# Ten weight-stationary matmul groups turned to activation-stationary, heads let in by the landing of their operands, and two output groups woven

## The chip, the cores and the metric

The kernel runs on one core of a Trainium2 chip. The metric is device time in microseconds (us) of one execution. In the rows, PE is the matrix engine and PEld its weight loads, DVE the vector engine, ACT the scalar engine, POOL and SPq two engines that here mostly issue DMAs; L95 is line 95 of the kernel before.

## The reference

Two layers over 256 positions of width 2048. A layer is one wide input projection, three kinds of head, a gate on each, one output projection and a layer norm:

```python
h = x @ w_in                       # (256, 2048) @ (2048, ...), split:
a_q, a_k, a_v, a_z, b_q, b_k, b_v, b_z, b_lr, m_q, m_z = jnp.split(h, cuts, axis=-1)
y_a = chunk_band_attention(a_q, a_k, a_v, rel_table)      # 8 heads of 128, softmax with a bias
o_b = gla_chunk_recurrence(b_q, b_k, b_v, log_g)          # 4 heads, gated linear attention, chunks of 64
y_b = o_b * lax.rsqrt(mean(o_b**2) + RMS_EPS) * gla_norm_g
y_m = memory_attention(m_q, *split(mem @ w_mem_kv))       # 4 heads of 128 into 256 memory rows
y = concatenate([y_a * silu(a_z), y_b * silu(b_z), y_m * silu(m_z)])
x = layer_norm(DEEPNORM_ALPHA * x + y @ w_out, ln_g, ln_b)
```

All arrays are float32.

## The kernel before

**Products.** Every big product is made in three parts, so as to keep float32 precision with inputs rounded for the matrix engine: an operand is split into `hi` (rounded) and `lo` (the rest), and the product is hi·hi + lo·hi + hi·lo. The activations are split once per layer into `x` tiles (`xq`: four quarters of the contracted dimension; a quarter holds hi and lo side by side, 2×256 columns).

**Pieces.** The weights are streamed. A `piece` is 2×128 rows of the contracted dimension by 512 columns, or 4×128 by 256: 128x1024 elements in a tile. SP loads it into a `raw` tile, ACT copies the rounded half to `wh` (L117), DVE subtracts and writes `wl` (L118). `raw`, `wh` and `wl` have four buffers each, so piece n can be split only when PE has done with piece n−4. The pieces carry a high priority for the scheduler that orders ACT, DVE and POOL; PE and SP run in the order in which the code is written.

**Two forms of a group.** A group is eight pieces, one tile of the PSUM (`acc`) and 512 output columns. `as_group` (activation-stationary): for each row block of 128 and each half of the 256 positions, three matmuls (hi·wh, lo·wh, hi·wl) with 512 weight columns streamed: a step of 3×512 columns. `ws_group` (weight-stationary): for each row block two matmuls of 512 columns (the stationary block of `wh` with hi and lo side by side) and two of 256 (`wl` with hi): a step of 2×512 + 2×256 columns. The weight-stationary form gives the result with channels on the partitions, which is what heads and gates want; the other gives positions on the partitions.

**Turning.** `turned` brings an activation-stationary result to channels on the partitions: DVE transposes 32x32 blocks into a scratch tile (L521), POOL sends it home to DRAM (L523) and reads it back block row by block row, four DMAs for each half (L526). `placed` then copies the landed blocks to their place. Before, the queries (AQ0, AQ1, MQ) take this way, the attention keys (AK0, AK1) and the gates (AZ0, AZ1, MZ) are weight-stationary, the gates with `total` (adding the two halves) and Silu.

**Order of work.** A layer is: memory keys and values; BQK; four value groups `values(0..3)` of 388 columns, with AQ0 and AK0 after `values(2)` and AQ1 and AK1 after `values(3)`; MQ; BZ; AZ0, AZ1, MZ; then four output groups WO. Beside the groups run the heads, written as Python generators: the linear attention (`gla`), eight attention heads (`a_head`: scores QK, bias, softmax, transposed probabilities `pT` by the way of `turned`, then PV on PE) and four memory heads (`m_head`, whose probabilities are also split, `sc<-pT`). `tick()` is called after each piece: it lets waiting heads in (two or three at a time) and runs a generator whose due time has come, at most one step each tick; a generator yields the number of ticks until it is due again. `finish(gens)` calls `tick` until those are done.

Of the kernel before, what the change touches and what calls it, by code (L numbers as in the profile page):

```python
# [8 lines left out]
F32 = mybir.dt.float32  # L9
# [27 lines left out]
def hybrid_trunk_kernel(  # L37
# [9 lines left out]


    ctx.enter_context(tc.manual_schedule(engines={PE, mybir.EngineType.SP}))
    waiting, active, done, now, linear = [], [], set(), [0], []  # L50
# [103 lines left out]
    def first_pieces(p, x):  # L154


        xsrc, j0 = memT[p // 2], p % 2 * 2
        xraw = early[:, p // 2]
        vsrc = w512[0, G_MV, p].rearrange("p (k n) -> p k n", k=2)
        ksrc = w512[0, G_MK, p // 2:8:4, :, j0 * 256:j0 * 256 + 512].rearrange("h p (k n) -> p k h n", k=2)  # L160
        raws, his, los = ([wp.tile([P, 2, 512], dt, name=nm(n), tag=n) for _ in range(2)]
                          for n, dt in (("raw", F32), ("wh", F32R), ("wl", F32R)))

        def x_part(j):
            sp.dma_start(xraw[:, j], xsrc[:, j])  # L165
            parts(x[0][:, j], x[1][:, j], xraw[:, j])

        def split(i, at):
            parts(his[i][at], los[i][at], raws[i][at])

        if p < 2:
            with tc.manual_schedule(engines={DVE, mybir.EngineType.Activation}):
                for k in range(2):
                    x_part(slice(j0 + k, j0 + k + 1))
                    cut = 2 if p == k == 0 else 1
                    for h in range(cut):
                        cs = slice(h * 512 // cut, (h + 1) * 512 // cut)
                        sp.dma_start(raws[0][:, k, cs], vsrc[:, k, cs])  # L178
                        split(0, (slice(None), k, cs))
# [12 lines left out]
    def first_memory(mk, mv, each):  # L192
# [5 lines left out]

        def values_of(p, w, kk):

            for h in range(2 if p == kk == 0 else 1):
                cs = slice(h * 256, h * 256 + 256) if p == kk == 0 else slice(0, 512)
                for t in range(2):
                    as_products(accv[:, t, cs], t, memq, [x[:, :, cs] for x in w], p * 2 + kk, kk, -1 if h else 0)

        def keys_of(p, w, kk):
            (wh, wl), (xh, _, both), j = w, memq[p // 2], p % 2 * 2 + kk
# [90 lines left out]
    def gla_inputs(l):  # L298

        gw = sm.tile([P, 256], F32R, name=nm("gw"), tag="gw")  # L300
        raw = hd.tile([48, 256], F32, name=nm("gwraw"), tag="pairs0")
        gb = small([P, 2], "gb")
        ng = small([P, 1], "ng")
        for i in range(3):
            pool.dma_start(raw[i * 16:i * 16 + 16], gate_w[l])  # L305
        pool.memset(gw.bitcast(F32), 0.0)
        tc.keep_in_program_order(act.copy(gw[:48], raw))
        tc.keep_in_program_order(dve.tensor_tensor(gw[32:48], raw[32:], gw[32:48].bitcast(F32), op=ALU.subtract))
        pool.dma_start(gb, gate_b[l])
        pool.dma_start(ng, norm_g[l])  # L310
        return gw, gb, ng

    def gla(gw, gb, ng, gq, gk, lr, asv, yraw):
# [178 lines left out]
    def gla_turned(yraw, ng, y):  # L492

        yT = []
        for par in range(2):
            yT.append(hd.tile([P, 4, P], F32, name=nm("yT"), tag=("gq", "gk")[par]))
            turned(P, (yT[par], yraw[:, 2 * par:2 * par + 2].rearrange("p t d -> p (t d)")))
            yield 6
        for par in range(2):
            for t in range(2):  # L500
                for b in range(2):
# [6 lines left out]
    def placed(raw, place):  # L508

        for t in range(2):  # L510
            place(raw[:, t].rearrange("p a (g j) -> p g a j", j=32),
                  lambda x: x[:, :, t * P:(t + 1) * P].rearrange("p g (a j) -> p g a j", j=32))
        return
        yield

# [14 lines left out]
    def a_head(h, load_bias, bias, q, k, asv, y):  # L530
# [1 line left out]
        if h + 2 < 8:  # L532
            load_bias(h + 2)
        pb = bank()
        mm(pb[:, 0:128], q[:, 0:128], k[:, 0:128], True, True)
        mm(pb[:, 128:384], q[:, 128:256], k, True, True)
# [238 lines left out]
    zeros = hd.tile([P, P], F32, name="zeros", tag="st")  # L775
    dve.memset(zeros, 0.0)
    idle = bank()
    for _ in range(6):
        mm(idle[:, :P], zeros, zeros, True, True)

    res = per.tile([P, 2, D], F32, name="res")
# [3 lines left out]
    for l in range(L):  # L785
        def halves(g):
            return [[w512[l, g, h * 4 + pc // 2][:, pc % 2 * 512:pc % 2 * 512 + 512] for h in range(2)] for pc in range(8)]

        def staged(g, x, raw, place):
# [3 lines left out]
            gen = placed(raw, place)  # L793
# [77 lines left out]
        for half in range(2):  # L871
            values(2 + half)
            q = hd.tile([P, 4, T], F32, name=nm("qk"), tag="qk", bufs=4)
            laid = staged(G_AQ0 if half == 0 else G_AQ1, xq, yraw[3], lambda src, at, q=q: act.copy(at(q), src))
            k = heads(G_AK0 if half == 0 else G_AK1)
            finish(laid)
            gens.append([a_head(half * 4 + h, load_bias, bias, q[:, h], k[:, h], asv, yraw[1 + half][:, h]) for h in range(4)])
            waiting.extend(gens[-1])
        q = [hd.tile([P, 4, T], F32R, name=nm("mq"), tag="qk", bufs=4) for _ in range(2)]
        laid = staged(G_MQ, xq, yraw[3], lambda src, at: parts(at(q[0]), at(q[1]), src))  # L880
        gens.append([m_head(h, q, mk, mv, yraw[3][:, h], laid) for h in range(4)])
        waiting.extend(gens[-1])


        acc = as_group(halves(G_BZ), xq, 512)
# [1 line left out]
        gla_gate(acc, yraw[0])  # L887
        yq = [operand()]
        gens[0] = [gla_turned(yraw[0], gp[2], yq[0])]
        waiting[:0] = gens[0]  # L890
        for i, g in ((1, G_AZ0), (2, G_AZ1), (3, G_MZ)):
            y = operand()
            gates = []
            for j, a, b in ws_group(w512[l, g], xq):
                sz = scratch([P, 2, T])
                total(sz, a, b)
                act.activation(sz, sz, AF.Silu)
                gates.append((j, sz))
            finish(gens[i])
            for j, sz in gates:  # L900
                dve.tensor_tensor(sz, sz, yraw[i][:, j:j + 2], op=ALU.mult)
                parts(y[0][:, j:j + 2], y[1][:, j:j + 2], sz)
            yq.append(y)
        finish(gens[0])


        last = l == L - 1
        stats = small([P, 2, 2 * WO_N, 6], "stats")
        gb = []
        rows = norm_rows(l) if last else None  # L910
        for n in range(WO_N):
            if last:
                g, b = scratch([P, 512]), scratch([P, 512])
            else:
                both = per.tile([P, 2, 512], F32, name=nm("gb"), tag=f"yr{n}")
                g, b = both[:, 0], both[:, 1]
            pool.dma_start(g, ln_g[l:l + 1, columns(n)].to_broadcast([P, 512]))
            pool.dma_start(b, ln_b[l:l + 1, columns(n)].to_broadcast([P, 512]))
            gb.append((g, b))
            src = wo_pieces(l, n)  # L920
            if last and n == WO_N - 1:

# [22 lines left out]

                norm_last(accs, rest, stats, gb, rows, more)
                break
            acc = as_group(src, yq, 512)
            for t in range(2):
                add_residual(n, t, acc[:, t], stats)  # L950
            if last:
                r = res[:, 1, columns(n)]
                dve.tensor_tensor(r, r, gb[n][0], op=ALU.mult)
        if not last:
            norm_between(stats)
            gbT = norm_columns(l)

# [85 lines left out]
```

## Time and profile before

| | |
|---|---|
| median of 3 runs (lowest, highest) | 910.96 us (910.96, 911.66) |
| the profiled execution | 911.12 us; its span 909.3 us, 1.8 us lie outside |
| granted PE clock | 0.998 of full speed |
| PE busy | 902.5 us, 99% of the span, 5116 instructions |
| DVE, ACT, POOL busy | 606.7, 486.0, 148.1 us |
| DMA | 200.86 MB, mean 221 GB/s |

The span is what the rows show, from the first instruction to the last. A row of a group of instructions is: line, engine, operation, out<-in with the shape of a tile, count | busy us, mean ns of one | idle us of that engine just ahead of them, and what ended it. A timeline row is: start us, duration us, engine, line, operation, count in the row, and in brackets the idle time ahead of it with its releaser.

### The profile page before, as it was taken

What the parts mean: (1) busy time and instruction counts of PE and PEld (TensorE: products, weight loads), DVE (VectorE), ACT (ScalarE), POOL (GpSimd) and SP (SyncE); (2) the same over time, 40 slices, a digit from 0 to 9 for tenths busy, and PEclk for the clock granted to TensorE, in tenths of its full rate; (3) what the DMA queues carried; (4) which work ended last, traced back from release to release, by engine and by line L of the source; (5) the groups of instructions that cost most, each with busy time, mean ns of one, the idle gap of its engine ahead of it and who ended that gap; (6) DMA issues with size and microseconds to landing.
All of it is one profiled execution on the core that took longest, in us unless ns stands there. A gap on an engine that the chain in (4) does not pass through costs nothing.

```text
span 909.3 us, 14115 instructions
## 1 busy us (share of the span) xinstructions
PE 902.5 (99%) x5116; PEld 783.0 (86%) x5116; DVE 606.7 (67%) x865; ACT 486.0 (53%) x708; POOL 148.1 (16%) x279
## 2 busy tenths in 40 slices
PE   9999999999999999999999999999999999999997
PEld 7889998998888888888888899889888888888885
DVE  5765478757566666655587676885756586876566
ACT  5654475474544666533476445754744365663340
POOL 1002002014142232000000220021141431420000
PEclk9999999999999999999999999999999999999999
DMA  8977875668786778756775687666696966696552
GB/s 292 315 229 213 303 222 185 184 206 272 213 238 215 234 221 257 229 197 195 225 249 177 197 242 209 195 195 208 193 282 192 271 208 212 209 295 212 190 162 93
DMA packets 109365, 200.86 MB, mean 221 GB/s; under 512 B 12136, under 2 KB 72936, under 8 KB 109040
## 3 DMA queue, kind: packets, MB, share of 16 engines
q1 hardware_dynamic: 97920, 173.31, 60.5%
q0 software_dynamic: 11232, 26.40, 10.2%
q8 instruction: 40, 0.66, 0.3%
q10 hardware_dynamic: 144, 0.26, 0.1%
q14 instruction: 29, 0.24, 0.1%
HBM read 186.78 MB, written 13.11 MB: 220 GB/s over the span
## 4 chain that ended last, share of the span: by engine, by line
PE 98%; DMA 1%; SPq 0%; DVE 0%; ACT 0%; issue 0%
PE acc L95 90%; PE bk L95 8%; DMA raw<-w 1%; PE bk L615 0%; SPq L178 0%; PE bk L398 0%; SPq L165 0%; ACT res L771 0%; ACT wh L117 0%; DVE stats L756 0%; PE bk L345 0%; SPq L180 0%; DVE res L755 0%; DVE res L707 0%; DVE mvt L710 0%
## 5 line engine op out<-in xcount | busy, mean ns | idle before, releaser
L95 PE MATMUL acc<-wh,x 128*128 128x512 f32 (+2 forms) x1812 | 538.8, 378 | 0.0
L118 DVE TENSOR_TENSOR wl<-raw,wh 128x1024 fp32r<-128x1024 f32 (+3 forms) x321 | 369.4, 1153 | 207.6 <-ACT wh L117 205.7
L117 ACT CAST wh<-raw 128x1024 fp32r<-128x1024 f32 (+3 forms) x321 | 318.5, 994 | 315.2 <-PE acc L95 244.9
L95 PEld LDWEIGHTS acc<-wh,x 128*128 128x128 f32 x1812 | 334.9, 189 | 48.9 <-issue 0.3
L95 PE MATMUL acc<-wl,x 128*128 128x512 f32 (+2 forms) x906 | 340.8, 376 | 0.0
L95 PE MATMUL acc<-x,wh 128*128 128x512 f32 x672 | 212.2, 397 | 0.1
L95 PEld LDWEIGHTS acc<-wl,x 128*128 128x128 f32 x906 | 170.5, 188 | 26.4 <-DVE wl L118 0.6
L95 PEld LDWEIGHTS acc<-x,wl 128*128 128x128 f32 x672 | 126.2, 188 | 29.7
L95 PE MATMUL acc<-x,wl 128*128 128x256 f32 x672 | 132.2, 278 | 0.0
L95 PEld LDWEIGHTS acc<-x,wh 128*128 128x128 f32 x672 | 103.7, 189 | 1.7 <-ACT wh L117 0.5
L523 POOL DMA_DIRECT2D home<-sc x46 | 25.7, 558 | 397.3 <-DVE sc L521 390.6
L526 POOL DMA_DIRECT2D pT<-home x96 | 52.6, 554 | 51.4 <-DMA home<-sc 29.9
L526 POOL DMA_DIRECT2D yr<-home x48 | 26.1, 551 | 15.1 <-issue 8.0
L545 ACT ACTIVATE sc<-sc,mx 128x128 f32<-128x128 f32 (+1 forms) x32 | 14.4, 450 | 17.2 <-DVE mx L543 17.2
L305 POOL DMA_DIRECT2D gwraw<-gate_w x6 | 3.1, 522 | 105.7 <-PE bk L603 104.9
L387 ACT ACTIVATE sc<-sc 128x512 f32<-128x512 f32 x12 | 7.6, 633 | 14.9 <-DVE sc L385 14.9
L521 DVE STREAM_TRANSPOSE sc<-sc 128x384 f32<-128x384 f32 (+1 forms) x24 | 14.9, 619 | 0.5
L538 DVE SCALAR_TENSOR_TENSOR sc<-bk,bias 128x384 f32<-128x384 f32 x16 | 8.7, 544 | 9.1 <-PE bk L95 9.1
L521 DVE STREAM_TRANSPOSE sc<-acc 128x512 f32<-128x512 f32 x18 | 11.8, 696 | 3.6 <-PE acc L95 3.4
L118 DVE TENSOR_TENSOR x<-sc,x 128x512 fp32r<-128x512 f32 x20 | 13.5, 685 | 0.7 <-ACT x L117 0.7
L526 POOL DMA_DIRECT2D qk<-home x24 | 13.1, 552 | 5.0 <-DMA home<-sc 5.0
L118 DVE TENSOR_TENSOR x<-res,x 128x512 fp32r<-128x512 f32 (+2 forms) x14 | 10.5, 765 | 5.1 <-ACT x L117 5.1
(211 smaller groups left out, 601.0 us busy)
## 6 DMA issues: line engine op xcount, KB each, us to landing
raw<-w SPq DMA_DIRECT2D x142, 512.0 KB, 4.4
raw<-w SPq DMA_DIRECT2D x227, 256.0 KB, 4.0
raw<-w SPq DMA_DIRECT2D x64, 388.0 KB, 3.7
home<-sc POOLq DMA_DIRECT2D x30, 256.0 KB, 4.0
bias<-relw SPq DMA_DIRECT2D x16, 192.0 KB, 4.7
yr<-home POOLq DMA_DIRECT2D x48, 64.0 KB, 4.9
home<-sc POOLq DMA_DIRECT2D x16, 192.0 KB, 3.3
pT<-home POOLq DMA_DIRECT2D x64, 48.0 KB, 4.3
```

The source lines that it names most:

```text
L95: pe.matmul(o, l, r, start=start, stop=stop, skip_group_check=True)
L117: act.copy(hi, src)
L118: dve.tensor_tensor(lo, src, hi.bitcast(F32), op=ALU.subtract)
L305: pool.dma_start(raw[i * 16:i * 16 + 16], gate_w[l])
L387: act.activation(dd, dd, AF.Abs)
L521: dve.transpose(blocks.rearrange("p b (g j) -> p g b j", j=32), src.rearrange("p (g b j) -> p g b j", b=4, j=32))
L523: pool.dma_start(homes[-1], blocks)
L526: pool.dma_start(dst[b * 32:(b + 1) * 32], home[:, b].rearrange("(a i) n -> i a n", a=4))
L538: dve.scalar_tensor_tensor(s, pb[:, :384], SCALE, bias[h], op0=ALU.mult, op1=ALU.add)
L545: act.activation(s[:, own[t]], s[:, own[t]], AF.Exp, bias=mx[:, t:t + 1], accum_out=zs[:, t:t + 1])
```

## The change

Five things change. (1) The keys AK0 and AK1 and the gates AZ0, AZ1 and MZ go from `ws_group` to `as_group` and `turned`: ten groups over the two layers. The keys are used as they land (`kv` is a view of the landed tile), with no copy; a gate goes through Silu on ACT straight from the PSUM, is turned, and is multiplied with the heads' result and split in the new `gated`. Their pieces come by two DMAs of 256 KB each in place of one of 512 KB. (2) `placed` and `gated` no longer run as one of the two or three generators let in: they stand in a list `side`, run at their due time (now six ticks after the group), and `placed` lets its heads in when it runs (`then`). (3) The first two output groups are woven: pieces 0 to 5 of the first, 0 to 5 of the second, then 6 and 7 of each; a gate must be done before the piece that reads it. (4) At the start, the first half of the first weights is issued on ACT's queue, the first part of the activations is split by DVE alone, the first piece's products are regrouped, and seven idle matmuls on zeros stand ahead instead of six. (5) The small inputs of the linear attention go from POOL's DMA queue to SP's, and in layer 0 the norm's `ln_g` and `ln_b` are loaded behind the output groups.

```diff
+        for e in [e for e in side if e[1] <= now[0]]:
+            side.remove(e)
+            after = next(e[0], None)
+            if after is not None:
+                side.append((e[0], now[0] + after))
+            else:
+                done.add(e[0])
...
         for i in range(3):
-            pool.dma_start(raw[i * 16:i * 16 + 16], gate_w[l])
+            sp.dma_start(raw[i * 16:i * 16 + 16], gate_w[l])
...
+    def gated(zT, yraw, heads, y):
+        while not all(h in done for h in heads):
+            yield 1
+        for j in range(0, 4, 2):
+            gz = scratch([P, 2, T])
+            for t in range(2):
+                z, o, r = (zT[:, t].rearrange("p a (k j) -> p k a j", j=32)[:, j:j + 2],
+                           *(x[:, :, t * P:(t + 1) * P].rearrange("p k (a j) -> p k a j", j=32) for x in (gz, yraw[:, j:j + 2])))
+                dve.tensor_tensor(o, z, r, op=ALU.mult)
+            parts(y[0][:, j:j + 2], y[1][:, j:j + 2], gz)
...
+        waiting.extend(then)      # at the end of placed
...
-    def m_head(h, q, mk, mv, y, laid):
-        while not all(g in done for g in laid):
-            yield 1
+    def m_head(h, q, mk, mv, y):
...
-            active.append((gen, now[0] + 5))
+            side.append((gen, now[0] + 6))
...
-            k = heads(G_AK0 if half == 0 else G_AK1)
+            k = hd.tile([P, 4, T], F32, name=nm("qk"), tag="qk", bufs=4)
+            kv = k.rearrange("p x y -> p (x y)").rearrange("p (ta g j) -> p g ta j", g=4, j=32)
+            gens.append([a_head(half * 4 + h, load_bias, bias, q[:, h], kv[:, h], asv, yraw[1 + half][:, h]) for h in range(4)])
+            landing = staged(G_AK0 if half == 0 else G_AK1, xq, k, None, gens[-1])
             finish(laid)
-            waiting.extend(gens[-1])
...
-            for j, a, b in ws_group(w512[l, g], xq):
-                sz = scratch([P, 2, T])
-                total(sz, a, b)
-                act.activation(sz, sz, AF.Silu)
...
+            acc = as_group(halves(g), xq, 512)
+            zT = hd.tile([P, 2, 4, P], F32, name=nm("zT"), tag="qk", bufs=4)
+            sz = [scratch([P, 512]) for _ in range(2)]
+            for t in range(2):
+                act.activation(sz[t], acc[:, t], AF.Silu)
+            turned(P, *((zT[:, t], sz[t]) for t in range(2)))
+            need[i * 2] = [gated(zT, yraw[i], gens[i], yq[i])]
+            side.extend((x, now[0] + 6) for x in need[i * 2])
...
+            order = [(m, pc) for pcs in (range(6), range(6, 8)) for m in accs for pc in pcs]
+            for m, pc in order:
+                finish(need.pop(pc, ()))
+                w = piece(wo_pieces(l, m)[pc], 512)
```

The scheduler's order moves with this at two places of each layer. The first is the end of the linear attention. On ACT, before (`yr_158` is its result, L475 its squares, `asv` the copy of `values(3)`, `wh_356` and `wh_359` the third and fourth piece of AQ1, the last load of a table that of the first head's exponentials):

```order
L470 COPY yr_158_1024<-bk_319_1910 64x512 x2
L117 CAST wh_356_2094<-raw_355_2093 128x1024
L475 ACTIVATE sc_317_1908,ms_316_1907<-yr_158_1024 128x128 x3
L117 CAST wh_359_2113<-raw_358_2112 128x1024
L475 ACTIVATE sc_317_1908,ms_316_1907<-yr_158_1024 128x128
L837 COPY asv_104_717<-acc_287_1735 128x2x388
L475 ACTIVATE sc_317_1908,ms_316_1907<-yr_158_1024 128x128 x2
L117 CAST wh_363_2136<-raw_362_2135 128x1024
L475 ACTIVATE sc_317_1908,ms_316_1907<-yr_158_1024 128x128 x2
L291 ACT_TABLE_LOAD
L291 ACTIVATE rs_u8_335_2015<-ms_316_1907,eps_91 128x8
L545 ACT_TABLE_LOAD
```

The same stretch of ACT now; here `wh_359` is the third piece of AQ1 and `wh_362` the fourth:

```order
L491 COPY yr_158_1025<-bk_314_1873 64x512 x2
L496 ACTIVATE sc_312_1871,ms_311_1870<-yr_158_1025 128x128 x6
L871 COPY asv_104_718<-acc_290_1723 128x2x388
L496 ACTIVATE sc_312_1871,ms_311_1870<-yr_158_1025 128x128 x2
L312 ACT_TABLE_LOAD
L312 ACTIVATE rs_u8_338_2003<-ms_311_1870,eps_91 128x8
L581 ACT_TABLE_LOAD
L581 ACTIVATE sc_325_1959,zs_327_1962<-sc_325_1959,mx_326_1961 128x128
L581 ACTIVATE sc_325_1959,zs_327_1962<-sc_325_1959,mx_326_1961 128x256
L124 CAST wh_359_2082<-raw_358_2081 128x1024
L124 CAST wh_362_2101<-raw_361_2100 128x1024
```

The casts of the third and later pieces, which stood between the copies and squares, now stand behind all of them, behind two table loads and the first head's exponentials.

The second place is the last gate group MZ. On ACT before (`sc_615` and `sc_620` are the split probabilities of memory heads 2 and 3; `wh_623` is the last piece of the first half of MZ, behind which PE makes head 2's PV, `wh_629` and the casts behind it are pieces of its second half; L262 and L897 belong to the gates):

```order
L117 CAST wh_623_3513<-raw_622_3512 128x1024
L262 ACTIVATE sc_606_3422<-acc_590_3324 128x512
L117 CAST sc_615_3478<-pT_576_3263 128x2x128 x2
L117 CAST wh_629_3548<-raw_628_3547 128x1024
L897 ACTIVATE sc_606_3422<-sc_606_3422 128x512
L117 CAST wh_633_3578<-raw_632_3577 128x1024
L117 CAST wh_636_3608<-raw_635_3607 128x1024
L117 CAST sc_620_3506<-pT_586_3311 128x2x128 x2
```

On ACT now (`wh_652` is the last piece of MZ, `wh_667` the first of WO, `sc_644` and `sc_649` the split probabilities of memory heads 2 and 3):

```order
L124 CAST wh_652_3554<-raw_651_3553 128x1024
L124 CAST wh_667_3606<-raw_666_3605 128x1024
L124 CAST wh_671_3632<-raw_670_3631 128x1024
L124 CAST wh_674_3650<-raw_673_3649 128x1024
L124 CAST wh_677_3668<-raw_676_3667 128x1024
L124 CAST sc_644_3522<-pT_602_3321 128x2x128 x2
L124 CAST sc_649_3547<-pT_612_3366 128x2x128 x2
L932 ACTIVATE sc_657_3582<-acc_623_3397 128x512
```

And on PE now, around memory head 2's PV (`bk_654`):

```order
L102 MATMUL acc_623_3397<-wh_652_3554,x_65_514 128x512 x2
L102 MATMUL acc_623_3397<-wl_653_3555,x_65_514 128x512
L102 MATMUL bk_654_3572<-sc_644_3522,mv_4_107 128x256
L102 MATMUL bk_654_3572<-sc_644_3522,mv_5_108 128x256
L102 MATMUL bk_654_3572<-sc_645_3523,mv_4_107 128x256
L102 MATMUL bk_654_3572<-sc_644_3522,mv_4_107 128x256
L102 MATMUL bk_654_3572<-sc_644_3522,mv_5_108 128x256
L102 MATMUL bk_654_3572<-sc_645_3523,mv_4_107 128x256
L102 MATMUL acc_664_3603<-wh_667_3606,x_505_2839 128x512 x2
L102 MATMUL acc_664_3603<-wl_668_3607,x_505_2839 128x512
```

The cast of head 2's probabilities stood right behind that of `wh_623`, the piece ahead of its PV. Now its PV stands behind `wh_652`, the last piece of MZ, and the cast stands behind those of four more pieces; the fourth, `wh_677`, takes the buffer of `wh_652`, which the matmuls just ahead of the PV read last. On DVE, in the same way, `wl_678` stands ahead of `sc_645`, the rest of those probabilities.

More of the change, by code (lines that the diff above doesn't have):

```diff
@@ L49, in hybrid_trunk_kernel @@
     ctx.enter_context(tc.manual_schedule(engines={PE, mybir.EngineType.SP}))
-    waiting, active, done, now, linear = [], [], set(), [0], []
+    waiting, active, side, done, now, linear = [], [], [], set(), [0], []
     def tick(share=1.0):
         now[0] += share
+        for e in [e for e in side if e[1] <= now[0]]:
[5 more added lines that the diff above has]
+                done.add(e[0])
         while True:
@@ L165, in x_part @@
             sp.dma_start(xraw[:, j], xsrc[:, j])
-            parts(x[0][:, j], x[1][:, j], xraw[:, j])
+            if p == j.start == 0:
+                dve.tensor_copy(x[0][:, j], xraw[:, j])
+                dve.tensor_tensor(x[1][:, j], xraw[:, j], x[0][:, j].bitcast(F32), op=ALU.subtract)
+            else:
+                parts(x[0][:, j], x[1][:, j], xraw[:, j])
         def split(i, at):
@@ L777, in hybrid_trunk_kernel @@
     idle = bank()
-    for _ in range(6):
+    for _ in range(7):
         mm(idle[:, :P], zeros, zeros, True, True)
@@ L787, in halves, with staged @@
             return [[w512[l, g, h * 4 + pc // 2][:, pc % 2 * 512:pc % 2 * 512 + 512] for h in range(2)] for pc in range(8)]
-        def staged(g, x, raw, place):
+        def staged(g, x, raw, place, then=()):
             acc = as_group(halves(g), x, 512)
@@ L792, in staged @@
             turned(P, *((raw[:, t], acc[:, t]) for t in range(2)))
-            gen = placed(raw, place)
-            active.append((gen, now[0] + 5))
+            gen = placed(raw, place, then)
+            side.append((gen, now[0] + 6))
             return [gen]
@@ L909, in hybrid_trunk_kernel, with load_norm @@
         gb = []
+        def load_norm(n):
+            for dst, src in zip(gb[n], (ln_g, ln_b)):
+                pool.dma_start(dst, src[l:l + 1, columns(n)].to_broadcast([P, 512]))
         rows = norm_rows(l) if last else None
@@ L912, in hybrid_trunk_kernel @@
             if last:
[L913 to L919, printed above, removed]
+                gb.append((scratch([P, 512]), scratch([P, 512])))
+                load_norm(n)
             src = wo_pieces(l, n)
```

87 lines of the change are left out of this document (51 added, 36 removed).

## The prediction

> **What bounds the kernel now.** I read the page first, then the chain of waits, then the waits by engine, and went to the timeline only at the places that the change touches. From the page and the chain:
>
> ```profile
> span 909.3 us, 14115 instructions
> PE 902.5 (99%) x5116; PEld 783.0 (86%) x5116; DVE 606.7 (67%) x865; ACT 486.0 (53%) x708; POOL 148.1 (16%) x279
> PE 98%; DMA 1%; SPq 0%; DVE 0%; ACT 0%; issue 0%
> ```
>
> And the whole list of what PE waited for, with one line of SP's:
>
> ```profile
> PE bk L95 <- DVE eps L784: 1.1, 1, 1.1
> PE bk L95 <- ACT nparts L117: 0.3, 1, 0.3
> PE bk L759 <- DVE nt L721: 0.3, 1, 0.3
> ...
> SPq L142 <- DVE wl L118: 366.8, 167, 5.3
> ```
>
> PE is the bound, and it waits 1.7 us in all: so the change can win only by PE work that goes away, and every microsecond for which another engine now makes PE wait is lost whole. SP stands waiting for free buffers for 366.8 us, so a few more issues on it are free; so are POOL's, busy 16% of the time, as far as no landing is late.
>
> **The gain: ten groups in the other form.** Both forms are in the trace. The group that goes has one row in the list of the costliest; 640 of its 672 matmuls are the ten groups' (64 each). A run of activation-stationary steps (three matmuls of 512), the first and last of 28 steps, and a run of weight-stationary ones (two of 512, two of 256), the first and last of 22:
>
> ```profile
> L95 PE MATMUL acc<-x,wh 128*128 128x512 f32 x672 | 212.2, 397 | 0.1
> ...
> 52.90 0.62 PE L95 MATMUL acc<-wh,x 128*128 128x512 f32 x2
> ...
> 71.94 0.62 PE L95 MATMUL acc<-wh,x 128*128 128x512 f32 x2
> ...
> 292.69 0.63 PE L95 MATMUL acc<-x,wh 128*128 128x512 f32 x2
> ...
> 308.02 0.63 PE L95 MATMUL acc<-x,wh 128*128 128x512 f32 x2
> ```
>
> (71.94 − 52.90)/28 = 0.680 us a step against (308.02 − 292.69)/22 = 0.697. A piece has four steps, so it goes from 2.787 to 2.720 us, and 10 groups of 8 pieces give 80 × 0.067 = 5.4 us less. This lies on PE, wholly on the path.
>
> [...]
>
> **What pays for the turning.** A turned result makes a trip that this trace shows for the queries, with the pace of the DMAs that bring it back, and the spread of landings for the probabilities:
>
> ```profile
> 150.21 1.13 POOL L523 DMA_DIRECT2D home<-sc  x2 [31.83 <-DVE sc L521]
> ...
> 154.43 4.35 POOL L526 DMA_DIRECT2D yr<-home  x8 [3.08 <-DMA home<-sc]
> ...
> yr<-home POOLq DMA_DIRECT2D x48, 64.0 KB, 4.9
> ...
> DMA to landing us min/median/max: 2.3/4.5/8.2
> ```
>
> From the first issue home to the last landing: 154.43 + 4.35 − 150.21 + 4.9 = 13.5 us, and some 1.5 us of transposes ahead. Heads enter six ticks later: 6 × 2.72 = 16.3 us. The keys are thus there about 1.5 us before they are asked for, at the least; the gates are asked for a group or more later. I put the trips at nothing; if a landing comes as late as 8.2 instead of 4.5, 3.7 − 1.5 = 2.2 us show.
>
> **What splits the pieces.** ACT casts a piece when PE has released a buffer, DVE subtracts:
>
> ```profile
> 223.49 1.05 ACT L117 CAST wh<-raw 128x1024 fp32r<-128x1024 f32 x1 [1.73 <-PE acc L95]
> 224.57 1.23 DVE L118 TENSOR_TENSOR wl<-raw,wh 128x1024 fp32r<-128x1024 f32 x1 [1.56 <-ACT wh L117]
> ```
>
> That is 2.3 us behind the release; PE needs it three pieces later, 3 × 2.72 = 8.2 us. So ACT and DVE may put just under 6 us of other work ahead of a piece before PE stops. This is the cover of all that follows, and the order of the changed kernel uses it up at two places of each layer.
>
> **First place: the end of the linear attention.** Rows of this stretch, ACT and DVE, then PE:
>
> ```profile
> 188.76 2.38 ACT L470 COPY yr<-bk 64x512 f32<-64x512 f32 x4 [0.62 <-PE bk L95]
> ...
> 192.27 0.30 ACT L475 ACTIVATE sc<-yr 128x128 f32<-128x128 f32 x1
> ...
> 192.70 0.31 ACT L475 ACTIVATE sc<-yr 128x128 f32<-128x128 f32 x1
> ...
> 194.81 0.81 ACT L837 COPY asv<-acc 128x776 f32<-128x776 f32 x1
> ...
> 198.05 1.28 ACT L291 ACT_TABLE_LOAD   x1
> ...
> 201.85 2.12 ACT L117 CAST wh<-raw 128x1024 fp32r<-128x1024 f32 x2
> ...
> 201.98 0.17 DVE L546 RECIPROCAL zs<-zs 128x2 f32<-128x2 f32 x1 [1.70 <-ACT sc L545]
> ...
> 204.78 1.21 DVE L118 TENSOR_TENSOR wl<-raw,wh 128x1024 fp32r<-128x1024 f32 x1
> ```
>
> ```profile
> 189.07 0.62 PE L95 MATMUL acc<-wh,x 128*128 128x388 f32 x2
> ...
> 193.41 0.63 PE L95 MATMUL acc<-wh,x 128*128 128x512 f32 x2
> ...
> 196.15 0.82 PE L95 MATMUL bk<-qk,qk 128*128 128x128 f32 x4
> ...
> 199.55 0.82 PE L95 MATMUL bk<-qk,qk 128*128 128x128 f32 x4
> ```
>
> Count from G = 189.07, where PE has left the linear attention and begins the last two pieces of `values(3)`. The changed ACT, before it casts AQ1's third piece (`wh_359`): copies end at 191.14 (G + 2.1); eight squares at 192.70 − 192.27 = 0.43 make 3.4; the `asv` copy 0.8; from the table load to the end of the first head's exponentials 201.85 − 198.05 = 3.8. So the cast starts at G + 10.1. DVE then has the same tail as in these rows ahead of `wl`, from the reciprocal to the end of the subtract: 205.99 − 201.98 = 4.0. `wl` is ready at about G + 14.2. PE, before its third matmul of that piece: 193.41 − 189.07 = 4.3 to the end of `values(3)`, two pieces each with a QK, 2 × 3.40 (199.55 − 196.15), the third QK 0.68 (3.40 − 2.72), two matmuls 0.45: G + 12.3. The wait is 1.9 us. Ends: 0.9, if the tail on DVE is a microsecond shorter (its norm work then needn't stand in it); 2.9 with as much on top. Two layers: **3.8 us** (1.8 to 5.8). Behind the cast stand head 1's exponentials, whose PV is not asked for until nine ticks later.
>
> **Second place: memory head 2's PV behind MZ.** The split of the probabilities:
>
> ```profile
> L117 ACT CAST sc<-pT 128x256 fp32r<-128x256 f32 x16 | 5.7, 403 | 6.8 <-DMA pT<-home 6.8
> L118 DVE TENSOR_TENSOR sc<-pT,sc 128x256 fp32r<-128x256 f32 x16 | 6.0, 419 | 3.6 <-ACT sc L117 3.6
> ```
>
> PE does this PV right after MZ's last piece. Now ACT has, ahead of the split, the cast of a piece (`wh_677`) into the buffer which that last piece only then releases, and DVE the subtract of the same piece. So PE comes to the PV and must see, from the release on: cast 1.05, subtract 1.23, two subtracts of the split 2 × 0.42: 3.1 us, less some 0.3 of matmuls that PE still has: 2.8 us. In layer 1 two gate products of the same shape stand ahead as well, 2 × 0.42: 3.6. Together **6.4 us**. The lower end is 2.2 for each, when PE's two matmuls on the first part of the split overlap the rest; the upper 4.5, when gate products wait for a landing in layer 0 as well: 4.4 to 9.0. This is a queue that depends on itself, no matter of a close race, and I hold it for the surer of the two. Head 3's split is behind it by 0.8 us with a piece between, and adds nothing.
>
> **The rest.** At the start PE waits for the first pieces:
>
> ```profile
> 1.05 2.93 PE L95 MATMUL bk<-zeros 128*128 128x128 f32 x12 [1.05 <-DVE eps L784]
> ...
> 1.18 0.89 SPq L178 DMA_DIRECT2D raw<-w  x2
> ...
> 3.58 5.77 DMA raw<-w
> ```
>
> One issue (0.89/2 = 0.45) leaves SP's queue; I take 0.3 us less (0.6 less to 0.4 more, if the seventh idle matmul stands in the way; six took 2.93 us). The inputs moved to SP and the norm's loads moved behind cost nothing beside 366.8 us of waiting. The weave has the same matmuls; the PSUM of the first output group comes free with two pieces, 5.4 us, still to go, and add_residual's few operations fit.
>
> Sum, against the profiled execution's 911.12 (span 909.3 and 1.8 around it): 911.12 − 5.4 − 0.3 + 3.8 + 6.4 = 915.6; the median of the runs shown is 0.16 lower, so **915.5 us**. With all low ends 911.12 − 5.4 − 0.6 + 1.8 + 4.4 = 911.3, with all high ends 921.0.
>
> **The rivals.**
>
> *No new wait* (0.09): 911.12 − 5.4 − 0.3 = 905.4, faster. It needs both queues to be shorter than I sum them, and is decided at the cast of `wh_677`: if the release of `wh_652` comes 3 us before PE ends MZ (its last reader is the last but one matmul by the order, which speaks against it), head 2's split is done in time; and at `wl_360`, where 2 us less must stand ahead. For it speaks that PE kept its cover at every place of before.
>
> *Only the wait behind MZ* (0.14): 905.4 + 6.4 = 911.8, no change to be told. The first wait is a difference of two sums of 12 and 14 us, and 2 us less of ACT work would remove it. *Only the first* (0.05): 905.4 + 3.8 = 909.2.
>
> *Late landings* (0.11): POOL now issues ten more trips; if the keys come 2.2 us late, or the pT queued behind them 3.7, once a layer: 920.0 to 923.0.
>
> *No gain in the form* (0.04): the step is set by the 1536 columns in both forms, so the 5.4 go: 921.0. The rows above speak against it; for it, that the weight-stationary run was taken where other work is woven in. [...]
>
> *The clock* (0.04): PE stops for 2 to 4 us, longer than any wait in the list of before, and may then be granted less than it is throughout before:
>
> ```profile
> core 0: 909.3 us, clock 0.998
> ```
>
> If half of a stretch like the idle matmuls' 2.93 us were lost after the longer wait of each layer, that is 2 × 1.5 = 3.0: 918.6. [...]
>
> **How the numbers follow.** The forecast, both waits, has 0.53, and its own range is the sum of the ends, 911.3 to 921.0. The range starts at 909.5, so that it takes in the case with the wait behind MZ alone (0.14), and ends at 921.0, which takes in the clock, the form without gain and the nearer part of the late landings. Left out: no new wait (0.09), the case with only the first wait (0.05) and half of the late landings (0.05). A measurement of this kernel can tell 0.2%, 1.8 us: faster is no new wait and half of the case with only the first, 0.12; the same (909.1 to 912.8) is the wait behind MZ alone and the low edge of the forecast, 0.15; slower is the rest, 0.73.
>
> **What would show it.** In the profile after: the group `acc<-x,wh` down from 672 matmuls to 32; PE's busy time down by about 5; new lines in PE's waits, for `wl` (two times, 1 to 3 us) and for `sc` by DVE (two times, 2 to 5 us), and ACT idle for PE right ahead of the cast behind MZ. If PE's list still holds only 1.7 us, the forecast is wrong and it is faster. If `qk` or `zT` landings stand in the list, it was the trips.

## The result: slower by 2.5%

The changed kernel takes 934.71 us (median of 5 runs, 931.61 to 935.94) against 911.62 (5 runs, 910.96 to 912.34): ratio 1.025, 95% interval 1.0233 to 1.0267. The forecast was 915.5 us, with a range of 909.5 to 921.0. The direction was right; the size was not, and the time lies far outside the range.

From the page of the changed kernel (profiled execution 934.89 us), the lines that answer to those shown of before:

```profile
span 933.1 us, 13853 instructions
PE 907.4 (97%) x4798; PEld 773.2 (83%) x4798; DVE 608.3 (65%) x878; ACT 483.0 (52%) x691; POOL 197.8 (21%) x369
PE 71%; issue 12%; DMA 9%; POOL 4%; ACT 2%; DVE 1%; SPq 0%; POOLq 0%; ACTq 0%; DVEq 0%
```

PE has 318 instructions fewer and is busy 4.9 us longer; the chain is PE's no more. What PE waited for (us in total, times, longest), and the granted clock of the core:

```profile
PE bk L102 <- DVE sc L125: 7.1, 2, 5.2
PE acc L102 <- DVE wl L125: 3.9, 2, 2.0
PE bk L102 <- ACT sc L124: 3.7, 3, 1.5
PE bk L102 <- DMA pT<-home: 3.5, 2, 3.4
PE bk L102 <- DVE eps L818: 1.1, 1, 1.1
PE acc L102 <- ACT wh L124: 0.8, 2, 0.5
...
core 0: 933.1 us, clock 0.987
```

That is 20.7 us of waits (with the two unchanged ones of 0.3 at the end), 19.0 more than before, and the clock is 0.987 where it was 0.998. Each wait has its place in PE's timeline:

```profile
201.69 0.50 PE L102 MATMUL acc<-wl,x 128*128 128x512 f32 x1 [1.96 <-DVE wl L125]
...
366.69 0.50 PE L102 MATMUL bk<-sc,mv 128*128 128x256 f32 x2 [1.52 <-ACT sc L124]
372.41 1.22 PE L102 MATMUL bk<-sc,mv 128*128 128x256 f32 x4 [5.21 <-DVE sc L125]
...
661.82 0.50 PE L102 MATMUL acc<-wl,x 128*128 128x512 f32 x1 [1.96 <-DVE wl L125]
...
690.89 1.62 PE L102 MATMUL bk<-pT,asv 128*128 128x256 f32 x4 [3.37 <-DMA pT<-home]
...
829.08 0.50 PE L102 MATMUL bk<-sc,mv 128*128 128x256 f32 x2 [1.52 <-ACT sc L124]
831.47 1.22 PE L102 MATMUL bk<-sc,mv 128*128 128x256 f32 x4 [1.88 <-DVE sc L125]
```

201.69 and 661.82 are the first place, AQ1's third piece; 366.69 to 372.41 and 829.08 to 831.47 are the second, memory head 2's PV behind MZ. 690.89 is new: the PV of attention head 2 in layer 1. In stretches of 2 us (stretch, its length, busy time of PE, PEld, DVE, ACT and POOL with their instructions, then the granted PE clock, the DMA share and GB/s) the two equal waits of 1.96 us end differently:

```profile
202.00:204.00 2.00, 2.00 (x7) 1.57 (x6) 1.86 (x3) 2.00 (x6) 0.00 (x0) 0.66 0.69 192
204.00:206.00 2.00, 2.00 (x6) 1.57 (x5) 1.96 (x4) 1.27 (x2) 1.65 (x4) 0.50 0.98 268
...
662.00:664.00 2.00, 2.00 (x10) 1.62 (x10) 1.95 (x3) 2.00 (x6) 0.00 (x0) 1.00 0.72 214
```

Behind the first the clock is halved until 206, and PE does 7 and 6 matmul records where it does 10 behind the second. Halved stretches stand at four of the five long waits (1.52 and 5.21 counted as one wait, 1.52 and 1.88 as another): 202.63 to 206.04, 369.89 to 376.72, 690.74 to 694.15 and 830.69 to 837.52. All four together:

```profile
sum 20.48, PE 17.04 PEld 14.02 DVE 13.97 ACT 6.13 POOL 7.65; mean PE 4.26 PEld 3.50 DVE 3.49 ACT 1.53 POOL 1.91
```

PE is busy there for 17.04 us. The clock's record is 0.50 in each, and a step of three matmuls takes 1.28 us (204.06 to 205.34) where it takes 0.68 at the full clock (208.20 to 208.88). If half of the 17.04 is put down to the clock, the halved clock costs an estimated 8.5.

| us | forecast | measured |
|---|---|---|
| form of ten groups, start | −5.7 | −3.6 |
| first place, both layers | +3.8 | +3.9 |
| second place, layer 0 | +2.8 | +6.7 |
| second place, layer 1 | +3.6 | +3.4 |
| other waits | 0 | +5.0 |
| halved clock | 0 | +8.5 (estimated) |
| sum | +4.5 | +23.9 (span 933.1 − 909.3 = 23.8) |

The −3.6 is PE's busy time without those 8.5, 898.9, against 902.5; three runs below with nearly the same instructions and no drop of the clock in their midst have 897.6 to 898.6, which would make it −4.9 to −3.9, and the clock's part 8.8 to 9.8. The other waits are 19.0 − 3.9 − 6.7 − 3.4.

### The profile page after: what moved, and what is told of

Read it like the earlier page. It is cut to its first block, busy times and chain, and to the rows that moved or that the text cites. A ratio compares the mean times of both kernels' runs of the same rounds, so it can differ in the third digit from the quotient of the medians.

```text
span 933.1 us, 13853 instructions
## 1 busy us (share of the span) xinstructions
PE 907.4 (97%) x4798; PEld 773.2 (83%) x4798; DVE 608.3 (65%) x878; ACT 483.0 (52%) x691; POOL 197.8 (21%) x369
## 4 chain that ended last, share of the span: by engine, by line
PE 71%; issue 12%; DMA 9%; POOL 4%; ACT 2%; DVE 1%; SPq 0%; POOLq 0%; ACTq 0%; DVEq 0%
PE acc L102 65%; PE bk L102 6%; DMA home<-sc 4%; DMA pT<-home 3%; POOL pT L561 2%; DMA zT<-home 1%; POOL home L558 1%; DMA yr<-home 1%; DMA raw<-w 1%; POOL yr L561 0%; POOL qk L561 0%; DVE wl L125 0%; ACT wh L124 0%; PE bk L649 0%; ACT sc L496 0%
## 5 line engine op out<-in xcount | busy, mean ns | idle before, releaser
L102 PE MATMUL acc<-wh,x 128*128 128x512 f32 (+2 forms) x2452 | 740.8, 383 | 0.8 <-ACT wh L124 0.8
L102 PEld LDWEIGHTS acc<-wh,x 128*128 128x128 f32 x2452 | 456.0, 189 | 75.1 <-ACT wh L124 1.3
L102 PE MATMUL acc<-wl,x 128*128 128x512 f32 (+2 forms) x1226 | 467.0, 381 | 3.9 <-DVE wl L125 3.9
L102 PEld LDWEIGHTS acc<-wl,x 128*128 128x128 f32 x1226 | 231.6, 189 | 44.4 <-DVE wl L125 5.2
L561 POOL DMA_DIRECT2D qk<-home x56 | 30.5, 553 | 19.6 <-DMA home<-sc 15.5
L561 POOL DMA_DIRECT2D zT<-home x48 | 26.2, 550 | 12.1 <-DMA pT<-home 5.6
L556 DVE STREAM_TRANSPOSE sc<-sc 128x512 f32<-128x512 f32 (+1 forms) x36 | 22.7, 642 | 3.5 <-ACT sc L932 2.1
L574 DVE SCALAR_TENSOR_TENSOR sc<-bk,bias 128x384 f32<-128x384 f32 x16 | 8.6, 538 | 20.7 <-PE bk L102 20.7
L102 PEld LDWEIGHTS bk<-pT,asv 128*128 128x128 f32 x64 | 12.4, 197 | 6.4 <-issue 3.8
L102 PE MATMUL bk<-pT,asv 128*128 128x256 f32 (+1 forms) x64 | 13.9, 342 | 3.5 <-DMA pT<-home 3.5
L124 ACT CAST x<-sc 128x512 fp32r<-128x512 f32 x20 | 11.8, 616 | 4.9 <-DVE sc L538 3.6
```

The lines of the kernel that those rows point to most:

```text
L102: pe.matmul(o, l, r, start=start, stop=stop, skip_group_check=True)
L124: act.copy(hi, src)
L556: dve.transpose(blocks.rearrange("p b (g j) -> p g b j", j=32), src.rearrange("p (g b j) -> p g b j", b=4, j=32))
L561: pool.dma_start(dst[b * 32:(b + 1) * 32], home[:, b].rearrange("(a i) n -> i a n", a=4))
```

## The experiments

The theory: two places in the queues of ACT and DVE make PE wait, and long waits are followed by a halved clock. The rivals: the trips through POOL are late whatever the order; or the clock falls for another reason and the waits alone count.

**Late gates.** The gates are let in three ticks later.

```diff
-            side.extend((x, now[0] + 6) for x in need[i * 2])
+            side.extend((x, now[0] + 9) for x in need[i * 2])
```

> One number of the changed kernel: the gates' products are let in nine ticks after their group, not six. In the order this puts the splits of memory heads 2 and 3 ahead of the casts that wait for a buffer, on ACT and DVE. Theory (the wait behind MZ is a matter of queue order, and the half clock follows each long wait): both waits behind MZ (6.7 and 3.4 us) go, and with them the 3.4 us that the lowered clock costs behind each: 934.7 - 10.1 - 6.8 = 917.8. Rival 1 (the trips through POOL are late, whatever the order): PE still waits for landings there, over 930. Rival 2 (the clock falls for another reason): only the waits go, 924.6, and the granted clock stays near 0.987.

Measured: 919.39 us, ratio to before 1.0084 (1.0066 to 1.0102), clock 0.996. From its list of PE's waits:

```profile
PE acc L102 <- DVE wl L125: 4.3, 2, 2.4
PE bk L102 <- DMA pT<-home: 2.3, 1, 2.3
...
PE bk L102 <- ACT sc L124: 0.7, 2, 0.4
```

The 7.1 us for DVE's split are gone, and so are the two drops behind them: the time falls by 15.3, where the waits alone (10.1) would have given 924.6. The theory holds within 1.6 us; both rivals miss.

**Queries and keys placed sooner.** Five ticks, as before the change, in `staged`.

```diff
-            side.append((gen, now[0] + 6))
+            side.append((gen, now[0] + 5))
```

> One number of the changed kernel: turned queries and keys are placed five ticks after their group, as before, not six, so heads enter one tick sooner. In the order the first head's exponentials now stand ahead of the linear attention's table load, one table load goes, and the casts of AQ1's pieces stand earlier on ACT. Theory: the two waits of 1.96 us at the end of the linear attention go, and the 1.7 us of half clock behind the first of them: 934.7 - 3.9 - 1.7 = 929.1. Rival 1 (trips too late for five ticks): the keys' landing shows instead, 934 or more. Rival 2 (clock for another reason): 930.8.

Measured: 930.35 us, ratio 1.021 (1.0192 to 1.0227). The two waits for `wl` at the first place are gone from the list, and so is the drop behind the first, as expected; a wait for `pT` of 0.97 us in layer 0 has come. The time alone does not tell the theory (929.1) from the rival for the clock (930.8).

**Both numbers.**

> Both numbers: five ticks for queries and keys, nine for the gates. Theory: the gains add, 934.7 - 16.9 - 5.6 = 912.2; if the late probabilities in layer 1 (3.4 us and 1.7 of clock) go as well, 907. Rival 1: 925 or more, new waits for landings. Rival 2: 920.7, with the clock at 0.987.

Measured: 917.15 us, ratio 1.0061 (1.0041 to 1.0082): 5 us more than the gains added. The timeline, of PE and in one row of ACT, says why (the profiled execution took 921.02 us, the longest of five):

```profile
227.73 0.89 PE L102 MATMUL bk<-pT,asv 128*128 128x256 f32 x4 [1.95 <-DMA pT<-home]
...
334.25 0.71 ACT L124 CAST sc<-pT 128x256 fp32r<-128x256 f32 x2 [3.86 <-DMA pT<-home]
335.01 1.22 PE L102 MATMUL bk<-sc,mv 128*128 128x256 f32 x6 [1.99 <-ACT sc L124]
...
683.09 1.62 PE L102 MATMUL bk<-pT,asv 128*128 128x256 f32 x4 [4.34 <-DMA pT<-home]
```

All three waits end with a landing of probabilities; the second is PE behind a cast of ACT, which itself stood 3.86 us for one. Heads let in one tick sooner ask for their probabilities sooner, and they are not there: here the rival of late landings is right. The tick that cures the first place costs at the PVs.

**What a wait costs beyond itself.** The kernel before, with PE made to wait 28 times for a short chain on DVE:

```diff
...
+            mm(b[:2, :2], eps, eps, True, True)
+            with tc.high_priority(3 * AHEAD):
+                t = small([P, 2], "stall")
+                dve.tensor_copy(b[:2, 2:4], b[:2, :2])
+                for _ in range(n - 1):
+                    dve.memset(b[:2, 2:258], 0.0)
+                dve.tensor_copy(t[:2], b[:2, 2:4])
+            mm(b[:2, 260:262], t[:2], t[:2], True, True)
...
```

> The kernel before, with 28 stalls put into it: at each, PE waits for a chain of a few small operations on DVE, 0.6 to 8 us; nothing else is changed. It measures what a wait costs beyond itself. Theory (from the changed kernel, where one wait of 1.96 us was followed by half clock and another of 1.96 was not, and those of 3.4 us and over all were): none below about 1.7 us is followed by a lowered clock, some near 2, all over 3.4; each such wait costs 1.7 or 3.4 us more. Rival (only the waits themselves cost, the clock is another matter): clock 0.998 as before throughout.

And the same with 32 waits, most of them of 0.8 to 3 us:

> The kernel before with 32 stalls of PE, most of them of 0.8 to 3 us, to see from which length on the clock drops. Theory from the first such run (none of 14 waits up to 1.20 us was followed by half clock, 13 of 14 from 1.77 us on were): none up to 1.2, nearly all from 1.8 on, and a share in between. Rival: a sharp bound.

Measured, one execution each: 1003.46 us with clock 0.973, and 1036.04 with 0.964. Two waits of the same length in the first of them, by their rows:

```profile
463.11 0.19 PE L112 MATMUL bk<-stall 2*2 2x2 f32 x2 [2.20 <-DVE stall L65]
...
944.47 0.19 PE L112 MATMUL bk<-stall 2*2 2x2 f32 x2 [2.20 <-DVE stall L65]
```

The first is followed by half clock, the second is not. Counted over both runs by PE's timeline and the clock in stretches of 2 us:

| wait of PE, us | waits | followed by half clock |
|---|---|---|
| 0.4 to 1.42 | 23 | 0 |
| 1.77 to 2.25 | 18 | 12 |
| 2.65 to 3.54 | 10 | 8 |
| 3.89 to 7.26 | 9 | 9 |

By the length of a wait there is no sharp bound between 1.8 and 3.5 us in these runs: the same 2.20 does and does not. The rival (clock as before throughout) is out.

The bound lies elsewhere. In every run the profile's clock records start each drop a whole number of steps of 3.413 us behind the drop before it (in the changed kernel 49, 94, 41 and 29, in the first of these two runs 9, 10, 11, 20, 36 and so on), and a drop lasts one step or two (the last in a run goes on past PE's work). By these records a step at half clock costs an estimated 1.7 us at most, half of 3.413. Cut into these steps, the two waits of 2.20 are not equal. These are the step with the most of each wait, and the step after it:

```profile
459.37:462.78 3.41, 1.54 (x9) 0.93 (x7) 2.42 (x5) 1.04 (x1) 0.00 (x0) 1.00 0.69 228
462.78:466.20 3.42, 3.09 (x9) 2.48 (x10) 0.28 (x2) 0.00 (x0) 0.00 (x0) 0.50 0.61 188
940.65:944.06 3.41, 1.62 (x9) 1.00 (x7) 2.42 (x5) 1.04 (x1) 0.00 (x0) 1.00 0.63 238
944.06:947.47 3.41, 3.00 (x15) 2.47 (x16) 0.35 (x2) 0.06 (x1) 0.00 (x0) 1.00 0.45 171
```

The first wait leaves PE idle for 3.41 − 1.54 = 1.87 us of one step, and the next step is halved. The second is cut by the border at 944.06; the fuller step has 3.41 − 1.62 = 1.79 us idle, and the clock stays. The same count over the steps of all 13 profiles, without the first step and the last 20 us of each:

| PE idle in a step at full clock, us | steps | next step at half clock |
|---|---|---|
| under 1.63 | 3323 | 0 |
| 1.63 to 1.87 | 12 | 3 |
| from 1.87 on | 39 | 39 |

A halved step was followed by another in all 12 cases with PE idle for 0.67 us or more, and in none of 42 with 0.36 or less. So these runs show a bound, and a nearly sharp one, between 1.63 and 1.87 us, a little over half a step; but it holds for PE's idle time in one step, not for one wait. In the changed kernel the wait that ends at 201.69 lies whole in a step (199.22 to 202.63), 1.96 us; the equal one that ends at 661.82 is cut at 660.02, which leaves 1.80. Short waits in one step add up: the step from 827.27 holds the 1.52 us and 1.1 of the 1.88 behind it, and the next is halved.

**The first place cured otherwise.** Late gates, and the last step of the linear attention two ticks later:

```diff
-        yield 2
+        yield 4
         rr = small([P, 8], "rr")
```

> The gates let in nine ticks after their group, and the linear attention's last step (root, two table loads and the scaling) four ticks after its squares in place of two, which also lets the first attention heads in later. In the order the casts of AQ1's pieces then stand ahead of the table loads and of the first head's exponentials. Theory: against the run with late gates alone (profiled 918.7) the waits of 1.96 and 2.37 us for AQ1's third piece go, the wait of 2.27 us for late probabilities too, since the heads move, and the 1.7 us of half clock: 918.7 - 6.6 - 1.7 = 910.4, or down to 906 where nothing else waits. Rival (the trips through POOL are the cause): other landings show, 914 or more.

Measured: 908.55 us, ratio 0.9964 (0.995 to 0.9978). No wait of PE over 1.14 us is left, and no drop of the clock before the end. Then with the memory heads' PV three ticks behind their split, in `m_head`:

```diff
-        yield 2
+        yield 3
         po = bank()
```

> As the run with late gates and the later last step of the linear attention, and the memory heads' PV three ticks behind the split of their probabilities in place of two. Theory: one more piece of cover for the split; the small waits for it (0.3 to 0.7 us) go: 0.7 to 1.5 us below that run, 906 to 909. Rival: no difference.

Measured: 907.87 us, ratio 0.9959 (0.9944 to 0.9975); not to be told from the run without it, and like that one 0.4% below the kernel before. Its page, list of waits, and clock:

```profile
span 905.9 us, 13854 instructions
PE 897.6 (99%) x4798; PEld 767.5 (85%) x4798; DVE 606.3 (67%) x878; ACT 480.7 (53%) x691; POOL 197.8 (22%) x369
...
PE acc L102 <- DVE wl L125: 1.5, 1, 1.5
PE bk L102 <- DVE eps L818: 1.1, 1, 1.1
...
core 0: 905.9 us, clock 0.998
```

The 1.5 us is again DVE standing before a gate's product for a landing (7.98 us, until 380.21), with a `wl` behind it. The norm's loads stand on POOL's queue just ahead of the gate's return, and the four transfers for which DVE waits take 7.5 us to land (median), so the loads were moved to SP in layer 0:

```diff
-                pool.dma_start(dst, src[l:l + 1, columns(n)].to_broadcast([P, 512]))
+                (pool if last else sp).dma_start(dst, src[l:l + 1, columns(n)].to_broadcast([P, 512]))
```

> The run with late gates, the later last step of the linear attention and the later PV of the memory heads, and in layer 0 the loads of ln_g and ln_b issued on SP and not on POOL, so that they no longer stand among the eight transfers that POOL has under way when the last gate's trip wants to go. Theory: the one wait left there (1.51 us, DVE's product of the last gate, whose landing waited for those loads) goes: 907.9 - 1.5 = 906.4, about 0.6% below the kernel before. Rival (the trip is late without them too): 907.9 as before.

Measured: 908.42 us, ratio 0.9962 (0.995 to 0.9975). The transfers now land in 4.0 us and the wait is gone, but others of 0.5 to 0.75 us stand in its profile, and the time is the same within the runs' spread: this expectation failed.

**The parts alone.** The keys as before, the gates turned:

> The changed kernel with the attention keys made as before (weight-stationary, heads let in as before); the gates, the weave and the rest as changed. In the order neither of the two bad places stands: the casts are interleaved at the end of the linear attention, and the heads' splits stand ahead of the casts that wait. Theory: six of the ten groups are won, 48 x 0.067 = 3.2 us, and no wait over 1 us: 908 to 909 and the clock at 0.998. Rival (the gates' trips are late in themselves): waits behind MZ as in the changed kernel, 920 or more.

Measured: 907.91 us, ratio 0.9962 (0.9949 to 0.9975). All that PE waited for there:

```profile
PE bk L102 <- DVE eps L818: 1.1, 1, 1.1
PE bk L102 <- ACT nparts L124: 0.3, 1, 0.3
PE bk L793 <- DVE nt L755: 0.3, 1, 0.3
PE acc L102 <- ACT wh L124: 0.2, 1, 0.2
```

So turned gates and the weave bring no wait by themselves, though the gates are let in after six ticks as in the changed kernel. Memory head 2's PV stands far ahead of MZ's end here (its Silu starts at 363.05):

```profile
346.93 0.89 PE L102 MATMUL bk<-sc,mv 128*128 128x256 f32 x6
```

The gates as before, the keys turned:

> The changed kernel with the gates made as before (weight-stationary); the keys turned, heads let in six ticks after, the weave and the rest as changed. Theory: four groups are won, 2.1 us; the two waits of 1.96 us at the end of the linear attention stay, the late probabilities in layer 1 too (0 to 3.4), one to three drops of the clock at 1.7, and about 1 us for memory head 2's split: 911.6 - 2.1 + 3.9 + 1 + (1.7 to 8) = 916 to 922. Rival (the keys have no part in it): 909.5.

Measured: 920.72 us, ratio 1.0109 (1.0086 to 1.0131): waits at the first place (1.58 us in layer 0, 1.33 in layer 1, where 1.96 were expected), of 2.48 and 2.82 us for `pT` in the two layers, and of 0.96 at the memory heads' split in each (the profiled execution took 924.51 us, the longest of four). Against the kernel before the keys alone lose 9.0 us and the gates alone win 3.8, but both together lose 23.1. So the 10 us behind MZ and their drops belong to neither part alone: by the rows, turned keys bring the memory heads' split behind MZ, and only turned gates put there a product that waits for a landing.

**The weave.** Gates turned, keys as before, and the first two output groups one after the other:

```diff
...
-            order = [(m, pc) for pcs in (range(6), range(6, 8)) for m in accs for pc in pcs]
+            order = [(n, pc) for pc in range(8)]
...
```

> The run with the keys made as before and the gates turned, and here the first two output groups unwoven: eight pieces of one, then eight of the other. Theory: with turned gates the weave is needed, since the last gate's trip of 15 to 19 us must be done before piece 6 of the first group, 16 us behind MZ; unwoven, PE waits 2 to 6 us for it in each layer, and the clock drops behind each: 907.9 + 4 to 12 + 3.4 to 6.8 = 915 to 926. Rival (the weave is worth nothing): 907.9.

Measured: 923.77 us, ratio 1.0138 (1.0121 to 1.0156), 15.9 above the woven run and as expected. PE stands for the last gate in both layers:

```profile
381.24 0.66 PE L102 MATMUL acc<-wh,x 128*128 128x512 f32 x1 [3.00 <-ACT x L124]
...
834.87 0.49 PE L102 MATMUL acc<-wh,x 128*128 128x512 f32 x1 [3.15 <-ACT x L124]
```

## Why the prediction was wrong, point by point

Of the 19.4 us between the forecast and the measured sum, 8.5 are the clock, 5.0 the other waits, 3.9 the second place of layer 0, and 2.1 the form and the start.

*The gain of the form* was right in kind: 5.4 forecast from the steps, 3.6 measured with the start in it, and 3.9 to 4.9 in the runs without a drop. *The start* gained nothing that shows; the 0.3 was too small to matter.

*The first place* was right to a tenth: 1.9 a layer forecast, 1.96 in each, and both ways of putting the casts earlier in ACT's queue took it away.

*The second place, layer 1*, was right (3.6, measured 1.52 + 1.88). *In layer 0* the term was mis-sized: 2.8, at most 4.5, measured 6.7. The step that failed is "I put the trips at nothing", with its reason that the gates are asked for a group or more later. PE needs the gates late, but DVE's queue holds the gate's product ahead of the piece's subtract and of head 2's split, so what waits for the landing is DVE, and PE behind it. DVE, then POOL, in the changed kernel, and the time that the first transfers of the gate's return took to land (how many, KB each, median us):

```profile
363.35 1.23 DVE L125 TENSOR_TENSOR wl<-raw,wh 128x1024 fp32r<-128x1024 f32 x1 [1.50 <-ACT wh L124]
369.78 0.76 DVE L538 TENSOR_TENSOR sc<-zT,yr 128x256 f32<-128x256 f32 x2 [5.21 <-DMA zT<-home]
370.46 1.22 DVE L125 TENSOR_TENSOR wl<-raw,wh 128x1024 fp32r<-128x1024 f32 x1
371.60 1.42 DVE L125 TENSOR_TENSOR sc<-pT,sc 128x256 fp32r<-128x256 f32 x4
```

```profile
353.75 1.13 POOL L558 DMA_DIRECT2D home<-sc  x2 [0.30 <-DVE sc L556]
358.97 2.19 POOL L561 DMA_DIRECT2D pT<-home  x4 [4.08 <-DMA home<-sc]
361.15 2.17 POOL L561 DMA_DIRECT2D zT<-home  x4
364.55 0.55 POOL L561 DMA_DIRECT2D zT<-home  x1 [1.23 <-DMA pT<-home]
...
zT<-home POOLq DMA_DIRECT2D x4, 64.0 KB, 6.8
```

The gate's data went home at 353.75, but its return stands behind head 3's `pT`, which waited 4.08 us for its own trip home, and DVE's product waits for the return's first four transfers, which take 6.8 us to land where 4.9 were taken: 369.78 − 353.75 = 16.0 us for half of a trip that was put at 13.5. (The last four, the first of which POOL issues only at 364.55, are read by products 5 us later.) That the product need not stand there is shown by the run with late gates, which has no long wait behind MZ. The margin of the keys was also mis-summed, 16.3 − 13.5 − 1.5 is 1.3 and not 1.5; no landing of keys stands in PE's list, so nothing hangs on it.

*Late landings* was a rival at 0.11 and came in part: 3.4 us in layer 1. POOL's rows there, and the times to landing of the send at 676.22 and of the fetch at 682.89:

```profile
676.22 0.56 POOL L558 DMA_DIRECT2D home<-sc  x1
681.62 1.09 POOL L558 DMA_DIRECT2D home<-sc  x2 [4.84 <-issue]
682.89 2.19 POOL L561 DMA_DIRECT2D pT<-home  x4 [0.18 <-issue]
...
home<-sc POOLq DMA_DIRECT2D x1, 192.0 KB, 6.1
...
pT<-home POOLq DMA_DIRECT2D x4, 48.0 KB, 6.0
```

Head 2's probabilities went home at 676.22 and landed 6.1 us later, at 682.3; over the whole run such a send takes 3.5 (median). They are fetched at 682.89, behind two sends home of MQ, so that place in the queue costs 0.6 us at most; the fetch takes 6.0 to land, against 4.7 over the run. The trip is late because both of its ways are slow. The DMA engines are full there (a share of 1.08 from 676 to 682); that this is the reason is not shown, since the runs that cured the wait moved the heads and not the load.

*The clock* was a rival at 0.04 and priced at 3.0. It is the largest part of what was missed: 8.5. Two things failed. The waits were summed as if they cost only themselves; and the 3.0 was an assumption, half of a stretch of 2.93 us behind the longer wait of each layer, since no row of before shows what such a wait costs beyond itself. The runs show drops after waits from 1.77 us on: PE idle for a little over half of one step of 3.413 us was enough (from 1.87 us on in 39 of 39 steps), and the steps keep their place from drop to drop through a whole run. With a drop at the 1.7 of one step behind each of the four waits of the forecast, 4 × 1.7 = 6.8, or 3.4 behind the two longer ones, 10.2, the sum would have been an estimated 922 to 926: still short of 934.7, by the late landings.

## What to carry to other kernels

Where the matrix engine hardly waits otherwise, a new wait of about 2 us can cost more than itself: in 12 of 18 waits of 1.77 to 2.25 us here half clock followed, at an estimated 1.7 us a step. Whether it does depends in these runs on where the wait falls in the steps of 3.413 us, so the same 1.96 us was dear in one layer and cheap in the next. None of 23 waits up to 1.42 us was followed by half clock, but 1.52 and 1.88 were, with 2.6 us of the two in one step. A result that its final user needs late can still stop an engine early, when the product that reads it stands in a queue ahead of urgent work (DVE stood 5.21 us for `zT`, and PE 5.21 us behind it); look at what is behind a waiting instruction, not only at who needs its result. Before blaming a queue for late data, compare each transfer's time to landing with its median (6.1 us against 3.5, where the place in the queue cost 0.6 at most). A tick's delay for a helper task is a knob on three queues at once: two such numbers turned +2.5% into −0.4%.

## What the runs showed of the hardware that I had not expected

The drops of PE's clock in the 13 profiles come in steps of 3.413 us that keep their place through a run: after a step at full clock in which PE was idle for 1.87 us or more the next was at half clock (39 of 39), after one with less than 1.63 it was not (0 of 3323), and between the two 3 of 12 were; a halved step with PE idle for 0.67 or more was followed by another (12 of 12), one with 0.36 or less was not (0 of 42). So waits as short as 1.77 us can be followed by half clock (12 of 18 waits of 1.77 to 2.25 us, none of 23 up to 1.42). A transfer's time to landing varies widely in one run: 6.1 us for a send of 192 KB whose median is 3.5. With four fetches of `pT` and four of `zT` issued from 358.97 on, POOL's ninth issue stood for 1.23 us, until 364.55, and the trace puts its release down to a landing of `pT`. In the run with late gates and the later PV the issues of the last two of the gate's eight fetches stood 0.77 and 1.90 us for the landings of the norm's two loads, issued eight places ahead of each. Why they stood is not shown.
